# A bidirectional encoder layer on one core: order of products, transposes and key/query work in the gated-linear-attention heads, and when sums made ahead are placed

## The chip, the cores and the metric

The kernel runs on one NeuronCore of one Trainium2 chip. A core has a matrix engine (TensorE, PE in the profile; its weight loads are listed apart as PEld), a vector engine (VectorE, DVE), a scalar engine (ScalarE, ACT), GpSimd (POOL), and SyncE (SP), which here only issues DMAs. Each engine works through its own instructions in order; semaphores tie the engines together. The metric is the time of one execution on the device in microseconds (us), lower is better.

## The reference

One layer over 512 tokens of width 2048 in float32. After an RMS norm, one projection feeds two halves: 16 heads of dilated window attention, and 4 heads of bidirectional gated linear attention (GLA) with key width 128 and value width 256. Their outputs are concatenated, multiplied by `w_out` and added to the input; then a SwiGLU block of width 5632 and a last norm follow. The change touches the GLA heads. Cut to them:

```python
G = cumsum(log_a)                       # per chunk, one gate for each direction
q_in = q * exp(G);  k_in = k * exp(-G)
A = (q_in @ k_in.T) * tril
intra = A @ v                           # within a chunk
U = (k * exp(G_last - G)).T @ v         # what a chunk adds to the state
S_prev = scan(state * decay + U)        # states before each chunk
o = intra + q_in @ S_prev
# once forward, once on the flipped sequence; the two are added, then
o = o * rsqrt(mean(o * o) + eps);  out = o * gla_norm_w * silu(gr)
```

The SwiGLU block computes `(silu(h @ w_gate) * (h @ w_up)) @ w_down`.

## The kernel before

**Large products.** float32 operands are split in two rounded parts, hi and lo, and a product takes three matmuls: hi·hi, hi·lo, lo·hi (lines 346 to 348). ACT rounds hi (L237), DVE forms lo (L218, "the rests"). The products with `w_gate` and `w_up` use a scheme with seven products of blocks in place of eight (`Feed`, from L1447), which needs sums and differences of blocks of the weights.

**Jobs.** The other large products run as a list of jobs. A job goes through its halves (a half is one block of 128 rows of a weight by 512 columns). In a half it visits four quarters, one for each block of 128 tokens, with three matmuls each into its own PSUM bank (8 banks in all; the running job holds four). The jobs around the change multiply by `w_out`: three with eight halves, called o1, o2, o3 here (columns 512 to 2047, the part of the attention heads), then o0 with sixteen halves (columns 0 to 511, all rows), then three more with eight halves. In the list of jobs, `n_in` is the place of o0, so o1 to o3 are `n_in-3` to `n_in-1`; `n_out` is that of the last one. At the end of a job DVE adds the four banks into the residual (L1304), which frees them.

**Side work.** After each quarter of these jobs the host program lets one step of side work issue its instructions (`run_side`). The four GLA heads are generators in that side work; two of them run staggered and take turns (`turns`, L753), one starting 12 turns after the other. A `yield` in `gla` (L913) ends a turn. While two heads run, a head has a turn every two quarters.

**A head**, `gla(h)`: the gates' logits on PE (L923); exponentials on ACT (L933 to L935); for each direction d a scan on DVE (L951), centring (L966), exponentials on ACT (L973 to L975), and `times(d)`, which multiplies the query's and the key's exponential by query and key (L982, DVE, two instructions). Then for each direction: four scores `a = ks·qs` (L1017, eight PE instructions), four transposes of the keys (L1020), a masked copy of the scores on DVE (L1023) into T, which POOL has zeroed (L1012), and a copy of the transposed keys on ACT (L1027). The two T are added (L1031). `sums(d)` multiplies keys and values (L1042), `decays(d)` scales on ACT (L1051), and `chain(d)` runs over the states on DVE (L1061, two dependent instructions for each direction). Then come the output products (L1089): for each block of 128 tokens T·v, queries times forward states, queries times backward states; 10 products or 20 PE instructions per head, into two banks. The block 0 needs the last backward state, block 3 the last forward one. Squares and the norm follow on ACT (L1097, L1105), transposes on PE (L1112) and the gate on DVE (L1115). Products, scores and states stay in plain float32, which takes two PE instructions each.

**Sums made ahead.** 21 blocks of sums of `w_gate` are made during o1 and the next jobs and stored in HBM for the later stage (`Feed.ahead`, L1472): a step reads 512 KB (issued on SP, L1404), four further steps are one DVE addition each (L1492), and then the block is stored (issued on POOL, L1494). After each half, `state["ahead"]` grows by the job's `ahead`, and for each whole unit one step is issued. 86 steps are needed in all.

**Queues.** All is issued in program order on each engine. DVE's queue holds the rests, the heads' work, the additions L1492 and the evacuations L1304 in one line; POOL's holds the stores L1494 and also the loads for the next heads (L850, L855), the residual's loads (L1257) and the zeroing of T.

Of the kernel before, what the change touches and what calls it, by code (L numbers as in the profile page):

```python
# [23 lines left out]
P = 128  # L24
# [88 lines left out]
def put(*slots):  # L113
    for s in slots:
        if s.home is not None:
            s.home.free.append(s.i)


def layer(nc, tc, x, attn_norm_w, w_in, rel_table, gw_f, gb_f, gw_b, gb_b, gla_norm_w, w_out,
# [4 lines left out]
    pe, act, dve, pool, sp = nc.tensor, nc.scalar, nc.vector, nc.gpsimd, nc.sync  # L124
    mm = pe.matmul

    with tc.manual_schedule(), \
# [7 lines left out]
        ps = Slots(pp, 8, 512, "ps")  # L135
# [23 lines left out]
        idn = cst.tile([P, P], F32, name="idn")  # L159
# [616 lines left out]
        gq, gk, gv = {}, {}, {}  # L776
# [136 lines left out]
        def gla(h):  # L913
# [15 lines left out]
            for d in range(2):  # L929
                tables(EXP_LN)  # L930
                bcol = wcol[:, (B_F, B_B)[d] + h:(B_F, B_B)[d] + h + 1]
                l, m = s2.get(), s2.get()
# [8 lines left out]
            gs, qs, ks = [], [], []  # L941
# [36 lines left out]
                ks.append(k)  # L978

            def times(d):  # L980
                for x_, y in ((qs[d], gq[h]), (ks[d], gk[h])):
                    dve.tensor_tensor(x_.t, x_.t, y.t, op=OP.mult)  # L982

            less(0)
# [24 lines left out]
            T, kt = [], []  # L1009
# [3 lines left out]
            for d in range(2):  # L1013
                a, tr = ps.get(), ps.get()
                for b in range(4):
                    c = slice(b * P, (b + 1) * P)
                    mm(a.t[:, c], ks[d].t[:, c], qs[d].t[:, c], start=True, stop=True)  # L1017
                for b in range(4):
                    c = slice(b * P, (b + 1) * P)
                    pe.transpose(tr.t[:, c], ks[d].t[:, c], idn)  # L1020
                put(ks[d])
                yield
                dve.copy_predicated(r3(T[d]), masks[:, d:d + 1, :].to_broadcast([P, 4, P]),  # L1023
                                    a.t.rearrange("p (b c) -> p b c", c=P))
                put(a)
                kk = s2.get()
                act.copy(kk.t, tr.t)  # L1027
                put(tr)
                kt.append(kk)
# [4 lines left out]
            v = [gv[h // 2][b // 2].t[:, b % 2, (h % 2) * 256:(h % 2 + 1) * 256] for b in range(4)]  # L1034
            S_ = [{}, {}]
# [21 lines left out]
            def chain(d):  # L1057
                for n, b in list(enumerate(orders[d]))[1:]:
                    at_ = b if d == 0 else b - 1
                    s = stts[d].t[:, n]  # L1060
                    dve.scalar_tensor_tensor(s, stts[d].t[:, n - 1], fs[d][:, at_:at_ + 1], s,  # L1061
                                             op0=OP.mult, op1=OP.add)
# [7 lines left out]
            decays(1)  # L1070
            yield
            chain(1)
            yield

            on = s4.get(F32, [P, 4, 256])
            ss, rs = cols[:, 8:12], cols[:, 12:16]
            junk = s2.get()
            os_ = []
            for i in range(2):
                o = ps.get()  # L1080
                for b in (2 * i, 2 * i + 1):
                    c = slice(b * P, (b + 1) * P)
                    ob = o.t[:, (b % 2) * 256:(b % 2 + 1) * 256]
                    terms = [(T[0].t[:, c], v[b])]
                    for d in range(2):
                        if b in S_[d]:
                            terms.append((qs[d].t[:, c], S_[d][b]))
                    for n, (l, r) in enumerate(terms):
                        mm(ob, l, r, start=n == 0, stop=n == len(terms) - 1)  # L1089
                os_.append(o)  # L1090
            put(T[0], *qs, *stts)
            if h % 2:
                put(*gv.pop(h // 2))
# [1 line left out]
            for b in range(4):  # L1095
                ob = os_[b // 2].t[:, (b % 2) * 256:(b % 2 + 1) * 256]
# [5 lines left out]
            for i in range(2):  # L1102
                for b in (2 * i, 2 * i + 1):
                    c = slice((b % 2) * 256, (b % 2 + 1) * 256)
# [4 lines left out]
            for i in range(2):  # L1109
                tr = ps.get()  # L1110
# [3 lines left out]
                o = s2.get()  # L1114
# [186 lines left out]
        def evac_out(c, part=False):  # L1301
            def f(banks):
                for t in range(4):
                    dve.tensor_tensor(x1[c][t].t, x1[c][t].t, banks[t].t, op=OP.add)  # L1304
                    put(banks[t])
                if not part:
                    urgent.append(rest())

            def rest():
                yield  # L1310
                for t in range(4):
                    squares(c, t, x1[c], ss2)
                    pool.dma_start(out=xd[4 * c + t], in_=x1[c][t].t)
                if c == 3:
                    dve.tensor_reduce(sum2, ss2.rearrange("p (t c) -> p t c", c=4), op=OP.add,
                                      axis=mybir.AxisListType.X)
                    rstd_of(sum2, 4, rstd2, 1.0 / D, scr)
                fs_ = {}
                for q in (2 * c, 2 * c + 1):
                    fs_[q] = s4.get(F32, [P, 2, 512])  # L1320
                    for k in range(2):
                        weighted(x1[c], 2 * q + k, W_FFN, fs_[q].t[:, k])
                    yield
                put(*x1.pop(c))
                if c == 3:
                    rb[2] = rows_of(rstd2)
                for q in (2 * c, 2 * c + 1):
                    yield from pair_operands(q, fs_.pop(q))
            return f
# [17 lines left out]
        def start_out(c):  # L1347
            def f():
                if c == 1:
                    free_h()  # L1350
                if c != 1:
                    load_res(c)
            return f
# [4 lines left out]
        def job_out(c, a, z, evac, **kw):  # L1358
            return job("B", [piece512(w_out, c * 512, k) for k in range(a, z, 2)], list(range(a, z)),
                       lambda k: mixh[k], evac, limit=3, **kw)  # L1360
# [9 lines left out]
        n_in = len(jobs)  # L1370
        jobs[n_front + 3].lead = lambda i: AHEAD + (i > 11) + (i > 13)
        j = job_out(0, 0, KT, evac_out(0), rate=RATES[1], start=start_out(0), before=load_first)
# [5 lines left out]
        for c in (1, 2, 3):  # L1378
            j = job_out(c, 8, KT, evac_out(c), rate=1.0, before=before_out(c))
        j.drop = drop_mix  # L1380

        n_out = len(jobs) - 1
# [380 lines left out]
        def evac_down(c):  # L1763

            def f(banks):
                for t in range(4):
                    y = s2.get()
                    act.activation(y.t, banks[t].t, AF.Copy, scale=rstd2[:, t:t + 1])
                    put(banks[t])
                    pool.dma_start(out=xd[4 * c + t], in_=y.t, accum_op=OP.add)  # L1770
                    put(y)
            return f
# [260 lines left out]
        for c in range(4):  # L2033
            j = job("B", [piece512(w_down, c * 512, k) for k in (0, 2)], list(range(4)),
                    lambda k: gT[k], evac_down(c), before=before_down(c))
# [6 lines left out]
        for c in range(4):  # L2042
            j = job("B", [piece512(w_down, c * 512, k) for k in (LAST - 4, LAST - 2)], list(range(LAST - 4, LAST)),
                    lambda k: gT[k], evac_later(c), before=before_later(c))
# [96 lines left out]
        run_last = finish()  # L2141
        state["sums"] = ff.ahead()
        for n, j in enumerate(jobs):
            j.ahead = {n_out: 0.0, n_out - 1: 1.0}.get(n, 2.0 if n_in <= n < n_out else 1.25 if n_in - 3 <= n < n_in else 0.0)
        for n, j in enumerate(jobs):
            if n == n_down:
                dn.run()
# [40 lines left out]
```

## Time and profile before

| | us |
|---|---|
| median of 3 runs (2168.88 to 2170.9) | 2170.3 |
| the profiled execution, whole | 2172.08 |
| its span, from the first to the last instruction | 2170.3 |
| ACT busy in the span | 1221.5 |
| POOL busy in the span | 355.6 |
| scores L1017, first and last start | 631.0, 722.7 |
| output products L1089, first and last start | 649.2, 739.0 |
| additions L1492, first and last start | 621.7, 815.4 |

How to read it: the profile has a start and a duration for each instruction, and what its engine waited for when it sat idle. A group row reads "line, engine, operation, tiles out<-in (buffer numbers left out: a and b are buffers in SBUF, ps is PSUM), shapes, count". A wait row reads "engine, what waited, <- who released it: total, times, longest". "PEclk" or the granted clock is the share of full speed that TensorE was given. Busy times of PE include matmuls that overlap, so two following matmuls start closer together than one lasts.

### The profile page before, as it was taken

What the parts mean: (1) busy time and instruction counts of PE and PEld (TensorE: products, weight loads), DVE (VectorE), ACT (ScalarE), POOL (GpSimd) and SP (SyncE); (2) the same over time, 40 slices, a digit from 0 to 9 for tenths busy, and PEclk for the clock granted to TensorE, in tenths of its full rate; (3) what the DMA queues carried; (4) which work ended last, traced back from release to release, by engine and by line L of the source; (5) the groups of instructions that cost most, each with busy time, mean ns of one, the idle gap of its engine ahead of it and who ended that gap; (6) DMA issues with size and microseconds to landing.
All of it is one profiled execution on the core that took longest, in us unless ns stands there. A gap on an engine that the chain in (4) does not pass through costs nothing.

```text
span 2170.3 us, 34929 instructions
## 1 busy us (share of the span) xinstructions
PE 2153.5 (99%) x12682; PEld 1900.2 (88%) x12682; DVE 1819.1 (84%) x3153; ACT 1221.5 (56%) x2228; POOL 355.6 (16%) x495
## 2 busy tenths in 40 slices
PE   9999999999999999999999999999999999999998
PEld 7888887888878889888888888888888899999987
DVE  6689996777768778899899998998999888898885
ACT  8455554677666446455555555555555655555562
POOL 0011213111011110011221212111221220021300
PEclk9999999999999999999999999999999999999999
DMA  6477779545475763467767677677776985576982
GB/s 202 137 179 181 180 183 250 151 139 174 142 256 181 246 230 120 134 181 182 187 176 185 181 181 195 171 186 178 178 199 176 267 205 175 180 182 157 282 309 78
DMA packets 264699, 405.71 MB, mean 187 GB/s; under 512 B 19341, under 2 KB 163389, under 8 KB 264526
## 3 DMA queue, kind: packets, MB, share of 16 engines
q1 hardware_dynamic: 206366, 274.59, 40.2%
q0 software_dynamic: 57840, 128.35, 26.5%
q8 instruction: 100, 1.64, 0.3%
q14 instruction: 73, 0.60, 0.1%
q10 hardware_dynamic: 320, 0.53, 0.1%
HBM read 287.47 MB, written 66.39 MB: 163 GB/s over the span
## 4 chain that ended last, share of the span: by engine, by line
PE 58%; DVE 0%; DMA 0%; issue 0%; ACT 0%; DVEq 0%; ACTq 0%
PE ps L1532 24%; PE ps L1518 12%; PE ps L1891 5%; PE ps L1890 5%; PE ps L1889 5%; PE ps L348 1%; PE ps L346 1%; PE ps L347 1%; PE ps L2085 1%; PE ps L2084 1%; PE ps L2086 1%; DMA gd<-b 0%; DVE b L1441 0%; DVE a L2117 0%; DVE a L1552 0%
## 5 line engine op out<-in xcount | busy, mean ns | idle before, releaser
L1436 ACT CAST b<-b 128x768 fp32r<-128x768 f32 (+1 forms) x569 | 519.2, 944 | 371.6 <-DVE b L1441 178.4
L1441 DVE TENSOR_TENSOR b<-b,b 128x768 fp32r<-128x768 f32 (+1 forms) x569 | 596.8, 1084 | 30.7 <-ACT b L1436 19.4
L1532 PE MATMUL ps<-b,b 128*128 128x512 f32 x1656 | 484.1, 393 | 0.4 <-ACT b L1436 0.2
L1532 PE MATMUL ps<-a,b 128*128 128x512 f32 x1368 | 401.1, 394 | 0.6 <-ACT b L1436 0.6
L1532 PEld LDWEIGHTS ps<-b,b 128*128 128x128 f32 x1656 | 280.8, 188 | 31.9 <-ACT b L1436 0.6
L1518 PEld LDWEIGHTS ps<-b,b 128*128 128x128 f32 x1656 | 271.4, 190 | 39.2
L1518 PE MATMUL ps<-b,b 128*128 128x256 f32 x1656 | 296.7, 280 | 0.0
L1518 PEld LDWEIGHTS ps<-a,b 128*128 128x128 f32 x1368 | 227.3, 189 | 37.2 <-DVE b L1441 1.0
L1532 PEld LDWEIGHTS ps<-a,b 128*128 128x128 f32 x1368 | 228.1, 189 | 23.0 <-ACT b L1436 0.8
L1518 PE MATMUL ps<-a,b 128*128 128x256 f32 x1368 | 245.6, 280 | 0.5 <-DVE b L1441 0.5
L1423 DVE TENSOR_TENSOR b<-b 128x512 f32<-128x512 f32 x260 | 177.9, 684 | 17.4 <-DMA b<-in_w_down_dram 6.5
L1889 PE MATMUL ps<-b,b 128*128 128x256 f32 x624 | 176.6, 283 | 0.0
L1890 PE MATMUL ps<-b,b 128*128 128x256 f32 x624 | 176.6, 283 | 0.0
L1891 PE MATMUL ps<-b,b 128*128 128x256 f32 x624 | 176.6, 283 | 0.0
L346 PE MATMUL ps<-b,b 128*128 128x512 f32 x304 | 122.7, 404 | 0.0
L1889 PEld LDWEIGHTS ps<-b,b 128*128 128x128 f32 x624 | 119.8, 192 | 0.0
L1890 PEld LDWEIGHTS ps<-b,b 128*128 128x128 f32 x624 | 119.8, 192 | 0.0
L1891 PEld LDWEIGHTS ps<-b,b 128*128 128x128 f32 x624 | 119.8, 192 | 0.0
L347 PE MATMUL ps<-b,b 128*128 128x512 f32 x304 | 119.2, 392 | 0.0
L348 PE MATMUL ps<-b,b 128*128 128x512 f32 x304 | 119.0, 392 | 0.0
L1424 DVE TENSOR_TENSOR b<-b,b 128x256 f32<-128x256 f32 x260 | 110.5, 425 | 9.0
L1425 DVE TENSOR_TENSOR b<-b,b 128x256 f32<-128x256 f32 x260 | 110.5, 425 | 8.9
(301 smaller groups left out, 4177.3 us busy)
## 6 DMA issues: line engine op xcount, KB each, us to landing
b<-in_w_gate_dram SPq DMA_DIRECT2D x109, 512.0 KB, 4.0
b<-in_w_up_dram SPq DMA_DIRECT2D x88, 512.0 KB, 3.9
b<-in_w_down_dram SPq DMA_DIRECT2D x88, 512.0 KB, 5.5
b<-a POOLq DMA_DIRECT2D x162, 256.0 KB, 4.6
b<-in_w_in_dram SPq DMA_DIRECT2D x78, 512.0 KB, 3.9
b<-in_w_out_dram SPq DMA_DIRECT2D x32, 512.0 KB, 5.1
gd<-b POOLq DMA_DIRECT2D x22, 512.0 KB, 4.0
b<-gd SPq DMA_DIRECT2D x22, 512.0 KB, 7.8
```

The source lines that it names most:

```text
L346: mm(o, xh.t[:, c], wh.t[:, w], start=first and not on, stop=False, skip_group_check=on)
L347: mm(o, xh.t[:, c], wl.t[:, w], start=False, stop=False, skip_group_check=on)
L348: mm(o, xl.t[:, c], wh.t[:, w], start=False, stop=last, skip_group_check=on)
L1423: dve.tensor_tensor(s_[:, :, 0:2], r[:, :, 1:3], r[:, :, 0:1].to_broadcast(shape), op=OP.add)
L1424: dve.tensor_tensor(s_[:, :, 2], s_[:, :, 0], r[:, :, 2], op=OP.add)
L1436: act.copy(o, src)
L1441: dve.tensor_tensor(o, src, h, op=OP.subtract)
L1518: mm(o, wl, xh, start=False, stop=end, skip_group_check=True)
L1532: mm(o.rearrange("p (s t) -> p s t", s=2), wh, x_, start=first and p == 0, stop=False, skip_group_check=True)
L1889: mm(o, xh[:, t], wh, start=first and h == 0, stop=False, skip_group_check=True)
L1890: mm(o, xh[:, t], wl, start=False, stop=False, skip_group_check=True)
L1891: mm(o, xl[:, t], wh, start=False, stop=last, skip_group_check=True)
```

## The change

Four edits:

1. `times(d)` multiplies the key first, then the query (before: query, then key).
2. For each direction the key's four transposes go to PE ahead of the four scores (before: behind them).
3. The output products are cut in two. T·v of all four blocks and the queries with the forward states go one turn earlier, right behind the call that issues the backward chain; the queries with the backward states stay in the turn in which all products were. The two PSUM banks are taken a turn earlier. The order of accumulation changes with it, and the start flag is set once for each bank.
4. The sums ahead: o1, o2, o3 add 0.5, 1.25, 1.5 steps for each half (before: 1.25 in each), o0 adds 2.25 (before: 2.0). Steps by job: 4 + 10 + 12 + 36 in place of 10 + 10 + 10 + 32.

```diff
             def times(d):
-                for x_, y in ((qs[d], gq[h]), (ks[d], gk[h])):
+                for x_, y in ((ks[d], gk[h]), (qs[d], gq[h])):
                     dve.tensor_tensor(x_.t, x_.t, y.t, op=OP.mult)
...
                 for b in range(4):
                     c = slice(b * P, (b + 1) * P)
-                    mm(a.t[:, c], ks[d].t[:, c], qs[d].t[:, c], start=True, stop=True)
+                    pe.transpose(tr.t[:, c], ks[d].t[:, c], idn)
                 for b in range(4):
                     c = slice(b * P, (b + 1) * P)
-                    pe.transpose(tr.t[:, c], ks[d].t[:, c], idn)
+                    mm(a.t[:, c], ks[d].t[:, c], qs[d].t[:, c], start=True, stop=True)
...
             chain(1)
+            os_ = [ps.get() for _ in range(2)]
+
+            def states(d):
+                for b in range(4):
+                    if b in S_[d]:
+                        mm(os_[b // 2].t[:, b % 2 * 256:(b % 2 + 1) * 256], qs[d].t[:, b * P:(b + 1) * P], S_[d][b],
+                           start=False, stop=d == (b < 3), skip_group_check=True)
+
+            for b in range(4):
+                mm(os_[b // 2].t[:, b % 2 * 256:(b % 2 + 1) * 256], T[0].t[:, b * P:(b + 1) * P], v[b],
+                   start=b % 2 == 0, stop=False, skip_group_check=True)
+            states(0)
             yield
...
-            os_ = []
-            for i in range(2):
-                o = ps.get()
-                for b in (2 * i, 2 * i + 1):
...
-                    terms = [(T[0].t[:, c], v[b])]
-                    for d in range(2):
-                        if b in S_[d]:
-                            terms.append((qs[d].t[:, c], S_[d][b]))
-                    for n, (l, r) in enumerate(terms):
-                        mm(ob, l, r, start=n == 0, stop=n == len(terms) - 1)
-                os_.append(o)
+            states(1)
...
-            j.ahead = {n_out: 0.0, n_out - 1: 1.0}.get(n, 2.0 if n_in <= n < n_out else 1.25 if n_in - 3 <= n < n_in else 0.0)
+            j.ahead = {n_out: 0.0, n_out - 1: 1.0}.get(n, (2.25 if n == n_in else 2.0) if n_in <= n < n_out else {0: 0.5, 1: 1.25, 2: 1.5}[n - n_in + 3] if n_in - 3 <= n < n_in else 0.0)
```

More of the change, by code (lines that the diff above doesn't have):

```diff
@@ L1077, in gla @@
             junk = s2.get()
-            os_ = []
-            for i in range(2):
-                o = ps.get()
-                for b in (2 * i, 2 * i + 1):
-                    c = slice(b * P, (b + 1) * P)
-                    ob = o.t[:, (b % 2) * 256:(b % 2 + 1) * 256]
-                    terms = [(T[0].t[:, c], v[b])]
-                    for d in range(2):
-                        if b in S_[d]:
-                            terms.append((qs[d].t[:, c], S_[d][b]))
-                    for n, (l, r) in enumerate(terms):
-                        mm(ob, l, r, start=n == 0, stop=n == len(terms) - 1)
-                os_.append(o)
+            states(1)
             put(T[0], *qs, *stts)
```

## The prediction

> **What bounds the kernel now.** I read the page first, for the busiest engine:
>
> ```profile
> PE 2153.5 (99%) x12682; PEld 1900.2 (88%) x12682; DVE 1819.1 (84%) x3153; ACT 1221.5 (56%) x2228; POOL 355.6 (16%) x495
> ```
>
> PE is busy 2153.5 of 2170.3 us, so nothing beside PE's own stream can be shortened to effect: what a reordering can win is the 16.8 us in which PE stands idle, and what the clock takes. Next, the waits of PE over the whole run (total us, times, longest us):
>
> ```profile
> PE ps L1089 <- DVE b L1061: 2.4, 3, 1.3
> PE ps L1017 <- DVE a L982: 1.8, 1, 1.8
> ...
> PE ps L1532 <- ACT b L1436: 0.8, 2, 0.6
> ...
> PE ps L1042 <- DVE b L1304: 0.4, 1, 0.4
> ```
>
> The two largest sit in the gated-linear heads, on the lines that the change touches: L1089 (output products) waits for L1061 (the chain over the states), L1017 (scores) waits for L982 (gate times query and key). Third, the stages, and with them the clock:
>
> ```profile
> 612.20:642.70 30.50, 28.68 (x132) 23.87 (x131) 21.64 (x41) 20.74 (x38) 7.46 (x15) 0.94 0.88 311
> 642.70:684.00 41.30, 39.36 (x190) 32.69 (x189) 33.84 (x67) 23.68 (x61) 8.13 (x16) 1.00 0.56 180
> 684.00:718.00 34.00, 33.10 (x164) 27.80 (x163) 30.19 (x63) 19.84 (x49) 5.10 (x10) 1.00 0.59 190
> 718.00:773.00 55.00, 55.00 (x266) 46.40 (x264) 34.06 (x77) 20.10 (x48) 7.10 (x15) 1.00 0.83 283
> ```
>
> Columns: stretch, length, busy PE, PEld, DVE, ACT, POOL, granted clock, DMA share, GB/s. The rows are jobs o1, o2, o3, o0, beside which the heads run. PE idles 1.8, 1.9, 0.9 and 0 us in them, and in o1 the clock is 0.94. Cut finer, at the clock's step:
>
> ```profile
> 628.36:631.77 3.41, 1.59 (x10) 1.11 (x9) 3.38 (x8) 2.75 (x6) 1.70 (x4) 1.00 1.07 373
> 631.77:635.19 3.42, 3.42 (x13) 3.00 (x13) 3.42 (x7) 0.63 (x2) 0.86 (x2) 0.50 1.07 380
> 648.84:652.25 3.41, 2.10 (x10) 1.50 (x9) 3.31 (x6) 1.75 (x4) 0.00 (x0) 1.00 0.92 338
> ```
>
> After 3.41 us with PE busy 1.59, the next 3.42 us ran at half clock; a stretch with 2.10 busy was not followed by that. So the wait for L982 is paid twice, as idle time and as half-speed matmuls.
>
> **The wait at head 0's scores.** The change does three things here: key before query in L982, transposes (L1020, key alone) before scores (key and query), and fewer sums (L1492) in DVE's queue. The timeline:
>
> ```profile
> 621.72 0.41 DVE L1492 TENSOR_TENSOR b<-b 128x256 f32<-128x256 f32 x1
> 622.05 0.68 DVE L945 TENSOR_TENSOR a<-a,a 128x512 f32<-128x512 f32 x1
> ...
> 628.90 0.88 DVE L1492 TENSOR_TENSOR b<-b 128x256 f32<-128x256 f32 x2
> 629.70 1.28 DVE L982 TENSOR_TENSOR a<-a,a 128x512 f32<-128x512 f32 x2
> ```
>
> ```profile
> 631.03 1.44 PE L1017 MATMUL ps<-a,a 128*128 128x128 f32 x8 [1.81 <-DVE a L982]
> ...
> 635.46 1.05 PE L1017 MATMUL ps<-a,a 128*128 128x128 f32 x8
> 636.36 0.60 PE L1020 MATMUL ps<-idn,a 128*128 128x128 f32 x4
> 636.71 0.47 PE L346 MATMUL ps<-b,b 128*128 128x512 f32 x1
> ```
>
> The scores wait for the second of two L982, the key's, done at 629.70 + 1.28 = 630.98. Keys first, that is one product earlier: 1.28 - 0.68 = 0.60, so 630.38. Ahead of the pair stand four L1492, steps 2 to 5 of the sums (the first row, one more like it, the two before the pair). At 0.5 a half instead of 1.25, o1's first four halves make two steps, a read and one L1492: three fewer, worth 0.33 (622.05 - 621.72) for each of two and half of 629.70 - 628.90 for the third, 1.06 together. ACT's exponentials and casts, which DVE follows there, may hold some of it; bounds 0 and 1.06, I take 0.9, since DVE is otherwise dense from 621.72 on. Then the key is ready at 629.5, where PE's last matmul ended at 631.03 - 1.81 = 629.22. The transposes go 0.3 late, last 0.35 to 0.45 (636.71 - 636.36 for four), and the query, 0.6 behind the key, holds the scores another 0.2. Of 1.8 idle 0.5 remains: **1.3 saved**.
>
> **The half clock.** From 631.03 to 635.46, 4.43 us, PE did one block of scores and transposes, which at full clock took 636.71 - 635.46 = 1.25, and two quarters of the job, six matmuls. A matmul of 512 columns steps by 0.23 (649.47 - 649.24, in a fence below), six by 1.4. So 1.8 were lost, against half of 3.42, 1.7. With 0.5 idle in place of 1.8 PE would be busy 2.9 of those 3.41, above the 2.10 that kept its clock: **1.7 saved**; bounds 0 (the half window stays) and 1.8.
>
> The Trainium skill, TensorE: Matmul & The Clock Gate, "HAM oscillation — how this bites in real kernels", asks only that PE has no idle gaps over about 3.4 us. The trace disagrees: a gap of 1.81 was followed by the half clock; by the rule its cause would be another and these 1.7 would stay, which is the second rival. Part 4 of that page, "PE-mode transpose", says that transposes don't count as PE activity for this gate, which speaks against putting them into the gap. By it the window would show 2.5 instead of 2.9, still above 2.10.
>
> **The products with the states.** Now T times v, forward and backward states go as 20 matmuls per head (two for each product) in one turn, and the second product already needs the end of the backward chain:
>
> ```profile
> PEld ps L1089 <- DVE b L1061: 3.6, 3, 1.7
> ```
>
> ```profile
> 646.86 1.06 DVE L1061 SCALAR_TENSOR_TENSOR b<-b,small 128x256 f32<-128x256 f32 x2
> ...
> 650.25 1.06 DVE L1061 SCALAR_TENSOR_TENSOR b<-b,small 128x256 f32<-128x256 f32 x2
> ```
>
> ```profile
> 649.24 0.39 PE L348 MATMUL ps<-b,a 128*128 128x512 f32 x1
> 649.47 0.59 PE L1089 MATMUL ps<-b,a 128*128 128x256 f32 x2
> 651.37 4.15 PE L1089 MATMUL ps<-b,a 128*128 128x256 f32 x18 [1.31 <-DVE b L1061]
> ```
>
> ```profile
> 735.10 4.48 PE L1089 MATMUL ps<-b,a 128*128 128x256 f32 x20
> 739.23 0.58 PE L346 MATMUL ps<-b,a 128*128 128x512 f32 x1
> ```
>
> Without a wait (last pair of rows, head 3) 20 take 739.23 - 735.10 = 4.13, 0.21 each. New order: 14 of them (T times v, forward) go a turn earlier, in head 0 six of the job's matmuls before 649.47, at 648.1; six stay. Do the 14 wait? T's sum is long done, and the forward states, after eight matmuls or 1.7 us, at 649.8, need a chain that ended at 647.92: no. Do the six wait? They are reached where the waiting product was (649.9) plus 12 x 0.21 = 2.5 of moved work, 652.4; the chain ended at 651.31, 1.1 to spare. PE will come earlier by what was saved ahead, but DVE's work there hangs on PE (the bank evacuations L1304, the next head's gates), so it comes earlier too. Saved: 3.6 of weight-load idle minus the normal step, 3 x 0.22: **2.9**; lower bound 1.5 beside a rival below. The matmuls are the same 20, and both banks are only held a turn longer; job ends (642.7, 684.0, 718.0, where four banks change hands) don't fall into that turn.
>
> **The second pair of sums' banks (L1042).**
>
> ```profile
> 641.34 0.75 DVE L1492 TENSOR_TENSOR b<-b 128x256 f32<-128x256 f32 x2
> 642.01 2.47 DVE L1304 TENSOR_TENSOR b<-b,ps 128x512 f32<-128x512 f32 x4
> ```
>
> ```profile
> 643.94 1.35 PE L1042 MATMUL ps<-b,a 128*128 128x256 f32 x5 [0.40 <-DVE b L1304]
> ```
>
> Head 0 waits for the evacuation at the end of o1, behind two L1492; at 0.5 a half one of them remains: **0.3 saved**.
>
> **What is added.** The copy of the scores (L1023) now waits for four transposes more, 0.35 to 0.45, while the transposed key's copy on ACT (L1027) starts earlier by the eight score matmuls, 0.9 (636.36 - 635.46). Behind L1023 on DVE stand the job's rests (L218), seven halves ahead of PE: nothing, at most 8 x 0.4 = 3.2 of DVE spread over four heads.
>
> The sums: the count of steps stays 86 (26 + 36 + 16 + 8 against 30 + 32 + 16 + 8). After o1 they are six behind, after o3 four, after o0 level. Each fourth add brings a 512 KB read on SP and a store on POOL:
>
> ```profile
> POOL sd L1494 <- DVE b L1492: 147.0, 20, 16.4
> ```
>
> ```profile
> L1404 SPq DMA_DIRECT2D b<-in_w_gate_dram x25: 367/368/2598, 612.4 to 832.9; - x25
> ```
>
> POOL is held by these stores, with the T memsets, the next head's loads and the residual loads behind them; in o1 that burden shrinks by two reads and two stores, at a DMA share of 0.88. Two more adds land in o3 (DVE 30.19 of 34.00) and four in o0 (34.06 of 55.00, PE without idle): 0.8 and 1.7 us of DVE, covered by 3.8 and 20.9 idle there. I charge **0.5 lost** for new small waits; bounds 0 and 1.7.
>
> **Sum**: 1.3 + 1.7 + 2.9 + 0.3 - 0.5 = 5.7. Behind o0 the program is unchanged and of PE's waits above only L1532's 0.8 lies there, so a gain there reaches the end. The profiled execution took 2172.08 (span 2170.3), and would take 2166.4; the median of the runs is 1.8 lower, 2170.3, and becomes **2164.6**. The three runs span 2.0 us, so the half window may be missing in the fastest.
>
> **Rivals.** First, DVE, not PE, sets head 0's end: it does not come earlier, and PE, however early, gets the last six products at 651.3. Then what was saved before head 0's chain is gone, and what remains is 12 x 0.21 = 2.5 there and 2.9 less head 0's 1.5 (1.7 - 0.22) at the other two heads: 3.9, 2166.4. For it: DVE is back to back from 641.34 on. Against it: L1304 waits for PE's job. Second, the half window stays, or the runs before didn't have it: 4.0, 2166.3. For it: the spread of the runs; against it, the 1.59 and 2.10 above. Third, the gain is given back at the start of the next stage, where PE waits for the splits already (L1532, 0.8) and the splits on ACT wait for a slot:
>
> ```profile
> ACT b L1436 <- DMA gd<-b: 6.6, 1, 6.6
> ```
>
> If that store doesn't move forward with PE, PE waits for it by as much as it came early: 2170.3. Against it: the store follows PE's own results. Fourth, slower: DVE in o3 is 89% busy and gets 0.8 more in less time. From the point where a head's products on DVE come 1.8 late, each head pays what head 0 pays now, 1.8 + 1.7 = 3.5; with three heads 10.5 against the 6.2 saved, 2174.6. Against it: DVE in o3 waits for PE, not PE for it, but for head 2's 0.9.
>
> **Numbers.** A run tells 0.2%, 4.3 us, from no change; faster means under 2166.0. The forecast, 2163.1 to 2166.4, has 0.55, of which 0.05 lies above 2166.0; first rival 0.16, second 0.13 (each a third under 2166.0, 0.1 together), third 0.08, fourth 0.08. Faster 0.5 + 0.1 = 0.6; same 0.05 + 0.19 + 0.08 = 0.32; slower 0.08. The range: from the whole 6.2 without the charge, less half the runs' spread, 2170.3 - 6.2 - 1.0 = 2163.1, up to the near edge of the third rival, 2170.3 - 1.0 = 2169.3; it leaves out the fourth and half of the third, and a little below.
>
> **What would show it.** The row of L1017 waiting for L982 gone or under 0.5; no stretch at clock 0.50 near 631; L1089's waits for L1061 gone, in two groups of 14 and 6; L1023's wait up, L1027's down; L1492 still 84, its first later. It is wrong if PE's idle in 612 to 718 stays over 2, or a new wait of PE shows behind 718.

## The result and the profile after

| | before | after |
|---|---|---|
| median, us (18 runs each) | 2170.41 (2168.45 to 2172.09) | 2165.98 (2165.16 to 2168.13) |
| ratio, 95% interval | | 0.9981 [0.9974, 0.9988] |
| the profiled execution, us | 2172.08 | 2165.94 |

The change saves 4.4 us in the medians, 0.2%, just at what a run can tell; in the two profiled executions it is 6.1. The page after, span and engines:

```profile
span 2164.2 us, 34918 instructions
...
PE 2151.6 (99%) x12682; PEld 1898.4 (88%) x12682; DVE 1820.8 (84%) x3153; ACT 1220.8 (56%) x2228; POOL 355.0 (16%) x495
```

Of the 6.1, PE's busy time gives 2153.5 - 2151.6 = 1.9 with the same number of matmuls (those of the half-clock stretch of before lasted longer), and its idle time 16.8 - 12.6 = 4.2. Of the waits of PE over the whole run, after, those that bear on the change (total us, times, longest):

```profile
PE ps L1017 <- DVE a L1115: 0.4, 1, 0.4
PE ps L1017 <- DVE b L1304: 0.3, 1, 0.3
...
PE ps L1532 <- ACT b L1436: 0.2, 1, 0.2
PE ps L1518 <- DVE b L1441: 0.2, 1, 0.2
PE ps L1017 <- ACT b L1105: 0.2, 1, 0.2
```

The chain L1061 and the product L982 are gone from the list. New are three waits of L1017, which are now the transposes (the line numbers of scores and transposes are exchanged): for a gate of another head (L1115), an evacuation at a job's end (L1304), a norm (L1105). None of these makes the transposes' operand; each frees a PSUM bank.

The run is best cut in three: the **heads' stage**, from o1's first matmul to the first of the job behind o0, and what lies ahead of it and behind. In windows (length, busy PE, PEld, DVE, ACT, POOL, clock, DMA share, GB/s), before:

```profile
612.20:773.00 160.80, 156.15 (x746) 130.76 (x744) 119.72 (x245) 84.36 (x195) 27.79 (x53) 0.99 0.72 242
773.00:1708.40 935.40, 933.85 (x5401) 820.99 (x5400) 843.84 (x1370) 515.20 (x891) 167.14 (x206) 1.00 0.68 179
```

and after:

```profile
612.80:768.00 155.20, 154.37 (x746) 129.17 (x745) 120.65 (x245) 84.17 (x195) 27.93 (x53) 1.00 0.74 251
768.00:1702.30 934.30, 933.65 (x5402) 820.92 (x5401) 844.16 (x1370) 514.82 (x891) 166.76 (x206) 1.00 0.68 179
```

The stage is 5.6 shorter: 1.8 less busy time (156.15 - 154.37), 3.8 less idle (4.65 to 0.83). The second stretch, up to the first product with `w_down`, in which the program is unchanged, is 1.1 shorter. The stage begins 0.6 later, for waits ahead of it that move from run to run (612.2 to 614.4 in the profiles of this study). 5.6 + 1.1 - 0.6 = 6.1. Because of that last term the experiments are read by the lengths of these two stretches first and by the medians second.

Head 0's first direction after, from the timeline:

```profile
618.66 0.75 DVE L936 TENSOR_SCALAR a<-ps,wcol 128x512 f32<-128x512 f32 x1 [8.30 <-ACT a L933]
...
621.13 0.74 DVE L936 TENSOR_SCALAR a<-ps,wcol 128x512 f32<-128x512 f32 x1
...
628.50 0.42 DVE L1492 TENSOR_TENSOR b<-b 128x256 f32<-128x256 f32 x1
628.83 1.29 DVE L982 TENSOR_TENSOR a<-a,a 128x512 f32<-128x512 f32 x2
...
629.42 0.39 PE L348 MATMUL ps<-b,b 128*128 128x512 f32 x1
629.65 0.60 PE L1017 MATMUL ps<-idn,a 128*128 128x128 f32 x4
...
630.17 1.16 PE L1020 MATMUL ps<-a,a 128*128 128x128 f32 x8
631.09 0.48 PE L346 MATMUL ps<-b,b 128*128 128x512 f32 x1
...
644.72 1.89 PE L1082 MATMUL ps<-b,a 128*128 128x256 f32 x8
646.44 1.46 PE L1078 MATMUL ps<-b,a 128*128 128x256 f32 x6
...
646.90 1.07 DVE L1061 SCALAR_TENSOR_TENSOR b<-b,small 128x256 f32<-128x256 f32 x2
...
649.12 1.46 PE L1078 MATMUL ps<-b,a 128*128 128x256 f32 x6
```

The transposes follow the job's matmul without a gap in which PE is marked idle; T·v and forward states go as 14, the backward states as 6 a turn later, 1.15 behind the end of the chain (646.90 + 1.07 = 647.97). And the window at the place where before ran at half clock:

```profile
631.77:635.19 3.42, 3.42 (x23) 2.97 (x22) 3.38 (x7) 1.39 (x4) 0.00 (x0) 1.00 1.03 383
```

PE is busy throughout, at full clock. What is not yet told is how much each edit gave, and whether the half clock belongs to a usual run of before.

### The profile page after: what moved, and what is told of

The parts are those of the page before. It is cut to its first block, busy times and chain, and to the rows that moved or that the text cites. A ratio compares the mean times of both kernels' runs of the same rounds, so it can differ in the third digit from the quotient of the medians.

```text
span 2164.2 us, 34918 instructions
## 1 busy us (share of the span) xinstructions
PE 2151.6 (99%) x12682; PEld 1898.4 (88%) x12682; DVE 1820.8 (84%) x3153; ACT 1220.8 (56%) x2228; POOL 355.0 (16%) x495
## 4 chain that ended last, share of the span: by engine, by line
PE 96%; DVE 2%; DMA 1%; issue 1%; ACT 0%; POOL 0%; DVEq 0%; ACTq 0%
PE ps L1532 31%; PE ps L1518 16%; PE ps L346 7%; PE ps L348 7%; PE ps L347 7%; PE ps L1891 5%; PE ps L1890 5%; PE ps L1889 5%; PE ps L339 1%; PE ps L337 1%; PE ps L338 1%; PE ps L663 1%; DMA b<-a 1%; PE ps L631 1%; PE ps L688 1%; PE ps L687 1%
## 5 line engine op out<-in xcount | busy, mean ns | idle before, releaser
L1436 ACT CAST b<-b 128x768 fp32r<-128x768 f32 (+1 forms) x569 | 519.0, 944 | 375.0 <-DVE b L1441 183.9
L1441 DVE TENSOR_TENSOR b<-b,b 128x768 fp32r<-128x768 f32 (+1 forms) x569 | 597.3, 1084 | 32.0 <-ACT b L1436 20.9
L1532 PE MATMUL ps<-b,b 128*128 128x512 f32 x1656 | 484.1, 393 | 0.4 <-ACT b L1436 0.2
L1532 PE MATMUL ps<-a,b 128*128 128x512 f32 x1368 | 401.1, 394 | 0.5 <-DVE b L1552 0.4
L1532 PEld LDWEIGHTS ps<-b,b 128*128 128x128 f32 x1656 | 280.8, 188 | 32.0 <-ACT b L1436 0.7
L1518 PEld LDWEIGHTS ps<-b,b 128*128 128x128 f32 x1656 | 271.4, 190 | 39.2
L1518 PE MATMUL ps<-b,b 128*128 128x256 f32 x1656 | 296.7, 280 | 0.0
L1518 PEld LDWEIGHTS ps<-a,b 128*128 128x128 f32 x1368 | 227.3, 189 | 36.9 <-DVE b L1441 0.6
L1532 PEld LDWEIGHTS ps<-a,b 128*128 128x128 f32 x1368 | 228.1, 189 | 23.1 <-issue 1.0
L1518 PE MATMUL ps<-a,b 128*128 128x256 f32 x1368 | 245.6, 280 | 0.2 <-DVE b L1441 0.2
```

The source lines that it names most:

```text
L1436: act.copy(o, src)
L1441: dve.tensor_tensor(o, src, h, op=OP.subtract)
L1518: mm(o, wl, xh, start=False, stop=end, skip_group_check=True)
L1532: mm(o.rearrange("p (s t) -> p s t", s=2), wh, x_, start=first and p == 0, stop=False, skip_group_check=True)
```

## The experiments

The edits have the numbers of the change: 1 and 2 the key's order (multiplied, transposed first), 3 the products in two turns, 4 the sums later. All ran on one chip in three sets (e1 to e4, e5 to e8, e9 to e12), each beside runs of before (medians there 2170.45, 2170.95, 2170.24, of 33, 26 and 29). The last column counts from the start of the job's last matmul ahead of a group of scores and transposes to the first one behind the group, added up over the eight groups (four heads, two directions), worked out from starts in the timelines.

| run (edits) | median us (n) | ratio to before, 95% | profiled us | stage | stretch behind | eight groups |
|---|---|---|---|---|---|---|
| before, first profile | 2170.41 (18) | | 2172.08 | 160.8 | 935.4 | 14.5 |
| e4 (none) | 2171.37 (11) | 1.0004 [0.9995, 1.0013] | 2171.43 | 159.0 | 935.3 | 13.7 |
| e1 (3) | 2167.81 (11) | 0.9988 [0.9979, 0.9996] | 2169.48 | 156.1 | 935.3 | 14.0 |
| e2 (1, 2) | 2170.88 (11) | 1.0002 [0.9993, 1.0011] | 2172.07 | 159.8 | 934.3 | 14.7 |
| e3 (4) | 2168.63 (11) | 0.9992 [0.9983, 1.0001] | 2168.68 | 157.4 | 934.4 | 12.4 |
| e5 (3, 4) | 2164.53 (7) | 0.9970 [0.9958, 0.9981] | 2165.22 | 154.2 | 934.3 | 12.4 |
| e6 (1, 2, 4) | 2168.57 (11) | 0.9991 [0.9982, 0.9999] | 2168.57 | 157.7 | 934.3 | 12.9 |
| e7 (1, 2, 3) | 2168.03 (11) | 0.9986 [0.9977, 0.9995] | 2168.08 | 157.0 | 935.2 | 15.0 |
| e8 (all, banks exchanged) | 2165.21 (9) | 0.9973 [0.9963, 0.9982] | 2165.72 | 154.4 | 934.5 | 12.7 |
| e9 (all) | 2166.39 (11) | 0.9983 [0.9974, 0.9992] | 2165.44 | 155.2 | 934.2 | 13.5 |
| e10 (3, 4) | 2165.17 (10) | 0.9978 [0.9969, 0.9988] | 2165.00 | 154.2 | 934.1 | 12.4 |
| e11 (all, banks exchanged) | 2165.36 (10) | 0.9977 [0.9967, 0.9986] | 2164.68 | 154.4 | 934.0 | 12.7 |
| e12 (3, 4 with later sums) | 2164.74 (9) | 0.9974 [0.9964, 0.9983] | 2164.71 | 153.8 | 935.0 | 12.3 |

Kernels with the same edits agree within 0.05 in the stage (e5 and e10, e8 and e11, e9 and the profile after), so a difference of 0.3 there is told apart; medians move by about 0.6 between sets. By the medians alone e2 and e3 are not told from before (their intervals hold 1), so the price of a part is read from the stage, and the medians bear it out only roughly.

**e4, before once more**, for the question whether the half clock is part of it.

> The kernel before, unchanged, for another profile. If the half window near 631 is there in each run, the profiled clock is 0.998 again and the span near 2170.3; if it is there in some runs only (the rival by which the usual run of before never lost these 1.7), a profile without it has clock 0.999 and a span near 2168.6, with the same 1.8 us of wait at L1017.

Windows of e4 (the stage, then the two around head 0's wait):

```profile
613.50:772.50 159.00, 154.46 (x745) 129.39 (x744) 119.68 (x245) 84.30 (x195) 27.68 (x53) 1.00 0.73 245
...
628.99:632.40 3.41, 1.73 (x9) 1.15 (x8) 3.34 (x9) 2.25 (x6) 1.19 (x3) 1.00 1.07 376
632.40:635.81 3.41, 3.41 (x26) 3.16 (x26) 3.41 (x8) 1.14 (x3) 1.36 (x3) 1.00 1.08 374
```

The same program, the same wait (1.7 for L982), PE busy 1.73 of 3.41 and then full clock. The stage is 1.8 shorter than in the first profile, and 1.7 of it is busy time (156.15 against 154.46): that is the half clock's price, and this execution didn't pay it. Each run also comes with its mean granted clock: the first profile of before has 0.998, e4's 0.999. Of the 33 runs of before in the first set, 24 have 0.999 (median 2170.4) and 9 have 0.998 (2171.8); all 18 of after have 0.999. A run without the half window is the usual one, and the median of before holds no price for it. (The granted clock also falls to 0.50 at the end of each run, when PE's work is over, 3.5 to 6.5 us ahead of the span's end in the 14 profiles; half of that over the span is 0.0008 to 0.0015 of the mean. A half window takes 1.7 / 2170, another 0.0008. So by this estimate a run at 0.999 had no such window, while 0.998 alone doesn't prove one: e10's profile has 0.998 from its end alone.)

**e1, edit 3 alone** (its lines of the change).

> Only the output products are cut in two (T times v and forward states a turn earlier); key, transposes and sums as before. Theory (three separate gains): PE's waits of L1089-type products for L1061 go from 2.4 us to under 0.3, the wait of the scores for L982 (1.8) and the half window near 631 stay; the time falls by 2.9 against before. Rival (DVE sets head 0's end): the six last products of head 0 still wait, head 0 gains 2.5, and the fall is the same or more, 2.5 to 3.9; no run here tells those apart but the wait of head 0's last six.

Windows of e1, the stage and then two that follow its wait at head 0:

```profile
614.40:770.60 156.20, 153.82 (x746) 129.68 (x745) 119.84 (x245) 84.45 (x195) 27.76 (x53) 1.00 0.74 249
...
631.50:634.91 3.41, 1.53 (x13) 1.53 (x14) 3.38 (x7) 2.66 (x6) 2.49 (x5) 1.00 1.07 369
634.91:638.33 3.42, 3.42 (x23) 3.03 (x22) 3.42 (x8) 1.13 (x3) 0.07 (x1) 1.00 1.06 388
```

Its largest wait of PE between 560 and 850:

```profile
PE ps L1017 <- DVE a L982: 2.0, 1, 2.0
```

No wait of L1078 or L1082 for L1061 is left, the stage is 2.9 shorter than e4's. With sums and key order as before, head 0's scores still wait 2.0, and again no half clock follows, with PE busy 1.53, less than the 1.59 of the first profile. That the half window near 631 stays, as was expected of this run, did not come; the wait for L982 and the gain of the products did.

**e2, edits 1 and 2 alone** (their lines of the change).

> Only key before query and transposes before scores. Theory: the key is ready 0.6 us earlier and the transposes fill 0.4, so PE's wait at head 0 falls from 1.8 to about 1.2 and the half window goes, since PE is then busy over 2.1 of 3.4 us: 1.0 of idle and, if the half window was there, 1.7 of clock; the wait of head 0's products for L1061 stays at 1.3 because DVE follows PE. Rival (DVE sets head 0's end): that wait grows by what was saved ahead, to 3 or more, and the time does not fall by over 0.5.

Timeline of e2 at head 0, and at the second direction of a later head:

```profile
632.05 1.29 DVE L982 TENSOR_TENSOR a<-a,a 128x512 f32<-128x512 f32 x2
...
632.79 0.66 PE L1017 MATMUL ps<-idn,a 128*128 128x128 f32 x4 [1.47 <-DVE a L982]
633.39 1.16 PE L1020 MATMUL ps<-a,a 128*128 128x128 f32 x8
...
694.37 0.40 PE L348 MATMUL ps<-b,a 128*128 128x512 f32 x1
695.13 0.66 PE L1017 MATMUL ps<-idn,a 128*128 128x128 f32 x4 [0.37 <-DVE a L1115]
```

The transposes do start with the first product, 0.74 into the pair. But the scores behind them have to wait for the second one (632.05 + 1.29 = 633.34, start 633.39), so only the four transposes have gone ahead: from the end of the pair to the job's next matmul pass 634.30 - 633.34 = 0.96, in e4 633.52 - 632.11 = 1.41, and 0.45 is won. (The whole group takes 3.37 against e4's 3.42, since DVE itself came 0.4 later here, for a wait that is told under e3.) And the later group pays for a bank: from 694.37 to 695.13 is 0.76 where two matmuls of a job start 0.23 apart. The wait at head 0 is 1.47 where 1.2 was expected, and the stage is 0.7 longer than e4's (159.76 against 159.04): these two edits lose. Head 0's products still wait 1.34 for L1061, so the rival, by which that wait grows to 3, did not come.

**e3, edit 4 alone** (the line of `j.ahead` as in the change).

> Only the sums ahead are set later. Theory: L982 of head 0 starts 0.9 earlier, so the scores' wait falls from 1.8 to about 0.9, the half window goes (1.7 if it was there), the wait for the banks falls by 0.3, L1061's waits stay: 1.2 to 2.9 less than before. Rival (the sums do not hold L982): the wait stays at 1.8 and the time within 0.5 of before.

Timeline of e3 at head 0:

```profile
629.21 1.29 DVE L982 TENSOR_TENSOR a<-a,a 128x512 f32<-128x512 f32 x2
...
630.55 1.16 PE L1017 MATMUL ps<-a,a 128*128 128x128 f32 x8 [0.37 <-DVE a L982]
```

The wait falls from 1.7 to 0.4 without any of the key's edits (0.9 was expected), and L1042's (0.3 to 0.4) is gone; the stage is 1.6 shorter. That is more than the additions: with the sums of before, ACT's cast ahead of head 0's second gate waits for a store that still reads its buffer, and DVE's L936 waits for ACT. Before, in the timeline:

```profile
618.08 0.75 DVE L936 TENSOR_SCALAR a<-ps,wcol 128x512 f32<-128x512 f32 x1 [8.30 <-ACT a L933]
...
619.81 0.62 ACT L237 CAST b<-b 128x512 fp32r<-128x512 f32 x1 [0.43 <-DMA gvd<-b]
...
621.05 0.75 DVE L936 TENSOR_SCALAR a<-ps,wcol 128x512 f32<-128x512 f32 x1 [0.42 <-ACT a L933]
```

The cast's wait for that store is 0.30 in e4, 0.69 in e2, 0.60 in e1, 0.35 in e7, and none in the kernels with the later sums. From head 0's first L936 to its first pair L982 pass 629.70 - 618.08 = 11.62 before and 628.83 - 618.66 = 10.17 after. Of these 1.45, 0.5 lie ahead of the second L936 (621.05 - 618.08 = 2.97 against 621.13 - 618.66 = 2.47), at this wait; 0.95 is additions. Over all the profiles the first part is 2.84 to 3.23 with the sums of before and 2.47 without that wait, so it is worth 0.4 to 0.8; the second, from that L936 to L982, is 8.64 with four additions ahead of L982, 7.7 with one and 7.36 with none (e12), whatever the other edits. How fewer sums free that buffer sooner is not shown.

**e5, e6, e7: one part undone each.** e5 is the whole without edits 1 and 2, e6 without 3, e7 without 4; the diffs are those above, backwards.

> The change without its first two edits: query before key and scores before transposes as before, products cut in two and sums later. Theory (the sums alone free L982; key first adds waits for banks of as much as it saves): the scores wait 0.4 for L982 as with the sums alone, the 0.9 of new waits of the transposes for banks (on L1115, L1304, L1105) is gone, and the time is within 0.5 of the whole change. Rival (key first is part of the gain): 1 us or more slower than the whole change.

> The change without the cut of the output products. Theory: the waits for L1061 are back at 2.4 us (3.6 of weight loads) and the time is 2.9 over the whole change, about 2168.9. Rival (DVE sets head 0's end): head 0's wait for L1061 is longer than the 1.3 of before, since PE comes 2 us earlier.

> The change without the later sums. Theory: the transposes of head 0 wait 1.2 to 1.5 for L982, the banks 0.3 for L1304, the products not; 1.6 over the whole change, about 2167.6. Rival (later sums are worth no more than 0.5 beside the other edits): within 0.5 of the whole change.

Stage of e5, in windows:

```profile
613.10:767.30 154.20, 153.76 (x746) 129.62 (x745) 120.45 (x245) 84.22 (x195) 27.95 (x53) 1.00 0.74 252
```

The products of e6 in its timeline, head 0:

```profile
648.10 1.13 PE L1089 MATMUL ps<-b,a 128*128 128x256 f32 x4 [1.33 <-DVE b L1061]
```

Each part can now be priced from several pairs that differ in it alone:

| part | pairs, change of the stage in us |
|---|---|
| products (3) | e4 to e1 -2.9; e3 to e5 -3.2; e2 to e7 -2.8; e6 to after -2.5 |
| sums (4) | e4 to e3 -1.6; e1 to e5 -1.9; e7 to after -1.8; e2 to e6 -2.1 |
| key's order (1, 2) | e4 to e2 +0.7; e1 to e7 +0.8; e3 to e6 +0.3; e5 to after +1.0 |

The signs hold in every pair. What spreads them is in part the cast's wait, which has moved by up to 0.4 between runs with the sums of before (from L936 to L936 2.84 in e4, 3.14 in e1, 3.23 in e2, 2.89 in e7, and 2.47 with the later sums). With these differences taken out, the sums give -1.3 in three pairs and -1.4 in one; the products -3.2 in both pairs with the old order of the key and -2.5 in both with the new; the key's order +0.3 in both pairs with the products in one turn, and +1.0 and +1.1 in those with two. So the parts add, but for 0.7 that the key's order and the products cost together. The group of transposes that waits for an evacuation L1304 holds most of it: it takes 2.03 in e7 and 2.00 after, and 1.48 in e2 and e6, which lack edit 3. That the products' banks, taken a turn earlier, leave these transposes another bank would fit; no run tests it by itself. The kernel without the key's edits is 1.0 shorter in the stage than the whole, so its expectation, within 0.5, fell short, and its rival (1 or more slower) had the wrong sign; where both ran in one set its median lies 1.2 below the whole's (e10 2165.17, e9 2166.39); the intervals of their ratios overlap. e6 speaks on the first rival: PE comes earlier there by what the sums save, and the wait for the chain doesn't grow (1.33, against 1.31 before), so DVE comes earlier with it. In e7 the transposes wait 1.14 for L982, and the stage is 1.8 over the whole's, close to what was expected.

**e8, e11: the banks exchanged.** `ps.get` hands out the bank that was put back longest ago. If the key's loss is the banks, and not the order on PE itself, giving the transposes, which now write first, the one that is handed out first should remove it.

```diff
-                a, tr = ps.get(), ps.get()
+                tr, a = ps.get(), ps.get()
```

> The whole change, and the transposes take the bank of the two that came free first, the scores the other (tr, a = ps.get(), ps.get()). Theory: the transposes' waits on L1115, L1304 and L1105 (0.9 us of PE) fall under 0.3, and the time by 0.6 to 1.0 against the whole change. Rival: the scores take over the same waits, and nothing moves.

> The whole change with the two banks swapped, again. Theory: under the whole change by 0.6 to 1.0 and, since no wait over 0.1 us of PE is left in the heads, no slower than the kernel without the first two edits. Rival: 0.5 or more slower than that kernel, by something that PE's waits in the heads don't show.

After, at a group that waits for an evacuation (timeline):

```profile
713.16 0.39 PE L348 MATMUL ps<-a,a 128*128 128x512 f32 x1
713.86 0.66 PE L1017 MATMUL ps<-idn,a 128*128 128x128 f32 x4 [0.31 <-DVE b L1304]
...
715.16 0.48 PE L346 MATMUL ps<-a,a 128*128 128x512 f32 x1
```

The same group in e8:

```profile
713.13 0.39 PE L348 MATMUL ps<-a,a 128*128 128x512 f32 x1
713.37 0.60 PE L1017 MATMUL ps<-idn,a 128*128 128x128 f32 x4
...
714.74 0.48 PE L346 MATMUL ps<-a,a 128*128 128x512 f32 x1
```

From matmul to matmul 2.00 after, 1.61 in e8, 1.48 where nothing waits. PE shows no wait at all in e8's heads, and its stage is 0.8 shorter than the whole's. The marked idle of 0.31 is only part of the price: the group loses 0.52, since the wait shows partly as a longer gap between matmuls that PE counts as busy. Hence the column of the eight groups: 8 x 1.48 = 11.8 would be without waits; after has 13.5, of which three groups (2.07, 2.00, 1.86) hold 1.5, and e5 has 12.4, of which head 0's first group (2.12) holds 0.64. The difference of 1.1 is the stage's 1.0. The order itself costs nothing: a group without a wait takes 1.48 either way round. The exchange removes 0.8 of the 1.5, as much as the stage gains; the three groups still take 1.68, 1.61 and 1.85, and PEld's waits there show the scores, which now take the later bank, waiting for L1105 (0.3) and L1115 (0.2).

**e9, e10**: the whole and e5 once more, beside e11 and e12.

> The whole change again, on the same chip as the next three. Theory (the first two edits cost about 1 us here): 2166.0, with the waits of the transposes on L1115, L1304 and L1105 of 0.9 in the profile. Rival (the difference to the kernel without them was the chip's): the median equals that of the kernel without them within 0.5.

> The change without its first two edits, again. Theory: 2164.5, 1 to 1.5 under the whole change; one wait of the scores for L982 of 0.4. Rival: within 0.5 of the whole change.

The order of the versions repeats, in stage and median. In this set the exchange (e11) is 1.0 under the whole and 0.2 above the kernel without the key's edits in the median, 0.8 under and 0.2 above in the stage.

**e12, the sums later still**: e5 with no step in o1.

```diff
-            {0: 0.5, 1: 1.25, 2: 1.5}[n - n_in + 3]
+            {0: 0.0, 1: 1.5, 2: 1.75}[n - n_in + 3]
```

> The change without its first two edits, and the sums later still: none in o1, 1.5 and 1.75 a half in o2 and o3. Theory (the sums ahead hold L982): the last 0.4 of wait at head 0's scores goes, 0.3 to 0.5 less than without this. Rival (DVE gets dense where the adds now fall, o2 and o3): a new wait of PE there, and the time equal or higher.

The stage of e12 in windows:

```profile
612.20:766.00 153.80, 153.77 (x745) 129.44 (x744) 120.59 (x245) 84.22 (x195) 27.77 (x53) 1.00 0.74 253
```

PE idles 0.03 in the whole stage: every wait in the heads that the change set out from is gone, and it is 1.4 shorter than the change's. In the median that is 2164.74 against 2166.39 in the same set; behind o0 it has 935.0, so it gives back 0.8 there, and over the two stretches together it is no better than e5 or e10 (1088.8 against 1088.5 and 1088.3). Its rival, a new wait of PE in o2 or o3, did not come.

## Why the prediction was right, and where it wasn't

The forecast fell 1.4 under the median (2164.6 against 2165.98) and 0.5 over the profiled time (2166.4 against 2165.94). Its sum of 5.7 came near the profiled difference of 6.1, in part by luck: the stage gave 5.6, but one of its parts met only in the whole (below), and of two terms that nothing in the sum stood for, 1.1 gained behind o0 and 0.6 lost ahead of the stage, one hid most of the other. Against the median, 1.7 of the sum is a half clock that a usual run doesn't have, and what came behind o0 makes up for part of it. Between faster (0.6) and no change that a run can tell (0.32) the result doesn't decide: the median lies 0.02 under the 2166.0 that was the limit, and the ratio's interval holds 0.998.

**Products, 2.9: right.** Measured 2.5 (with the new order of the key) to 3.2 (with the old), in two groups of 14 and 6, and the chain ends 1.15 ahead of the six, where 1.1 was worked out. The products themselves wait for neither bank. That the banks "are only held a turn longer" was put at nothing, and by itself it cost nothing (e1 and e5, all groups behind head 0's first take 1.47 or 1.48); with the key's edits a wait of 0.5 comes with it (L1304, above).

**Half clock, 1.7: right in size, wrong in place.** The two executions of before differ by 1.8 in the stage, 1.7 of it busy time, so the price was real in the profile that the sum was made against. The step that failed is the one that carried it over to the runs: "the median of the runs is 1.8 lower, 2170.3, and becomes 2164.6" keeps the 1.7 in a median whose runs mostly don't have that window. Without it the sum is 4.0, which is the second rival's 2166.3, 0.3 from the measured median, in the half of it that said the runs before didn't have it. The ground given, "PE would be busy 2.9 of those 3.41, above the 2.10 that kept its clock", was sound as far as it went: in no profile was a stretch with over 1.59 followed by half clock. What it didn't ask is whether a wait of 1.8 lowers the clock in each run; in e4 and e1 waits of 1.7 and 2.0 didn't (the last section reads the clock's stretches in them).

**The wait at head 0, 1.3, the banks of L1042, 0.3, and the charge: the whole met by luck, its parts mis-sized.** 1.3 + 0.3 - 0.5 is 1.1, and of the 3.9 from e4's stage to the one after, 1.0 is left beside 2.9 for the products. Sums were put at 0.9 + 0.3 = 1.2 and gave 1.6 to 2.1: the additions 0.95 and L1042 0.3 to 0.4, both as forecast, and 0.4 to 0.8 from ACT's cast behind a store, which the profile of before showed (the row with 0.43 above) and the sum left out. The key's order, which with what the sums leave of the wait was to add 0.4 (1.3 - 0.9), did win that at head 0: from the old to the new order its group is 0.42 to 0.45 shorter in all four pairs, once the cast's wait is taken out (0.64 to 0.19 over a plain 1.48 from e5 to after). What failed is that the sum asked when each operand is ready and not which bank it goes to. At three other groups 1.5 was lost, so that the key's order cost 0.3 to 1.0 in all.

**The charge of 0.5 for new small waits: right that there are some, too small**, and not where I looked (copies, POOL). Three banks cost the 1.5; without edit 3, two cost 0.9 (e2 and e6). The signs named also erred there: L1027's wait fell, as said, but L1023's fell as well, in place of rising. DVE's and ACT's waits before:

```profile
DVE a L1023 <- PE ps L1017: 2.6, 2, 1.6
ACT a L1027 <- PE ps L1020: 10.8, 6, 3.0
```

and after:

```profile
DVE a L1023 <- PE ps L1020: 1.1, 2, 0.9
ACT a L1027 <- PE ps L1017: 4.4, 3, 1.5
```

Why L1023's wait fell is not shown; its two waits before (1.02 at 636.62, 1.57 at 662.69) follow scores that PE reached late.

**Behind o0, nothing forecast, 1.1 gained.** The third rival expected the gain to be given back at the start of the next stage; the opposite came, in the same place. The part of the second stretch in which PE idles, before:

```profile
850.00:912.00 62.00, 60.45 (x440) 56.58 (x439) 51.95 (x96) 35.91 (x63) 0.54 (x1) 1.00 0.35 105
```

and after, over the same 440 matmuls:

```profile
845.00:906.00 61.00, 60.37 (x440) 56.70 (x439) 52.15 (x96) 35.91 (x63) 0.54 (x1) 1.00 0.34 107
```

The stretch is 1.0 shorter, nearly all of it idle (1.55 to 0.63); the waits of L1532 for L1436 (0.8 to 0.2) and of L1518 for L1441 (0.5 to 0.2) are its largest pieces. Kernels with it are after, e2, e3, e5, e6 and e8 to e11; without it are before, e4, e1, e7 and e12. With the key's edits or the sums alone it comes, yet not in e7, which has the keys, nor in e12, whose sums are the latest. So no single edit sets it, but the traces show where it lies: ACT's wait of L1436 for the store `gd<-b`, the one that the third rival named, is 5.1 to 5.5 in the nine kernels with the gain and 6.2 to 6.6 in the five without. In all fourteen that store is issued 122.2 after the stage's end; L1436 starts 5.7 to 6.1 later in the nine and 6.8 to 7.2 in the five. So the store came forward with PE, and was besides done sooner. Why it is done sooner, and whether that belongs to the change at all, is left open.

**Fourth rival, slower: no.** After, no score, transpose or product waits for DVE's L982 or L1061 in o3; of the three banks one (L1115, at 689.5) lies there, and e2, with the sums as before, waits for it as well (695.13).

So the accounts of a usual run, e4 to after: products -3.2, sums -1.3, the cast's wait -0.4, key's order +0.3, products and key's order together +0.7 make -3.9, as the stages have it (159.04 to 155.17); with 1.0 behind o0, whose cause is open, 4.9, beside 4.4 in the medians.

## What to carry to other kernels

Read the same kernel's profile twice, or its granted clock in the other runs, before a price that shows in one execution is taken off the median of many. When instructions of one engine change places, ask not only when each operand is ready but which PSUM bank each one gets and who frees it last: moving the first writer onto the later bank cost more than the earlier operand won. And a reordering that brings one operand forward wins no more than the work that can go before the other is needed: 0.45 here, of the 0.6 by which the key was earlier.

## What the hardware showed beside this

**The half clock follows PE's busy time in stretches of a fixed grid, with an edge near 1.6 of 3.41.** The granted clock falls to 0.50 once more at the end of each run, when PE's work is over. In the first profile of before (columns as above):

```profile
2160.95:2164.36 3.41, 0.96 (x9) 0.75 (x7) 3.00 (x11) 1.37 (x7) 0.00 (x0) 1.00 0.00 0
2164.36:2167.77 3.41, 0.00 (x0) 0.00 (x0) 1.55 (x4) 0.00 (x0) 0.00 (x0) 0.50 0.72 261
```

From the half stretch's begin at 631.77 to this fall at 2164.36 are 1532.59, which is 449 times 3.4133. Counted back in the same steps from the falls of e4 (2165.02) and e1 (2164.08), the stretches with the wait begin at 629.02 and 631.50, so those shown for them above lie on the grid, to 0.03. Read on this grid, a stretch with PE busy 1.47 or less was followed by half clock at the end of each run (0.96 above, 1.47 in e10 from 2153.30), and so was the one with 1.59 in before. After 1.73 (e4, at the wait), 1.91 and 2.01 (e7 and e1, near their ends) and all that have more, the clock stayed. Only the 1.53 of e1 that kept it stands out of this order. So the edge lies near 1.6 of 3.41 as far as these profiles tell, and PE's busy time, whose ends are modelled, does not place it better. The waits of before and e4, 1.81 and 1.68, lie whole within one stretch and leave 1.59 and 1.73, close on both sides of that edge; a wait across a border of the grid is shared, as e2's 1.47, which leaves 3.04 and 2.31 in the two stretches that it touches. That the same program loses the clock in one run and keeps it in another would fit this; no run tests it by itself. The Trainium skill, TensorE: Matmul & The Clock Gate, "Part 1: The HAM clock gate (the "warmup" mystery)", says that the gate watches a free-running window of 3413 ns, whose place against the kernel varies from run to run. The traces agree: steps of 3.4133 us, and a grid whose borders lie elsewhere in each profile (631.77 in before, 632.43 in e4).

**A wait for a bank costs more than its idle time says.** The group at 713.16 had 0.31 marked as idle and lost 0.52; the sum over three such groups was 0.84 marked (0.37 + 0.31 + 0.16) and 1.5 lost.
